# Two-layer hybrid trunk on one core: the weight sums of six P pairs of layer two formed next to their products instead of being read from a copy in DRAM

## The chip, the core and the metric

The kernel runs on one core of one Trainium2 chip. The metric is the device time of one execution in microseconds (us). Five engines work side by side, each through a list of instructions of its own, in order: PE (TensorE, the matrix products), DVE (VectorE), ACT (ScalarE), POOL (GpSimd) and SP (SyncE). SP and POOL do nothing here but start DMA transfers, so a transfer that must wait for its place holds up every transfer that stands behind it on the same engine.

## The reference

Two layers work on x of 2048 tokens by 1024 channels, all in float32. Cut to what matters:

```python
for l in range(DEPTH):                      # DEPTH = 2
    shift, scale, gate = jnp.split(silu(c) @ w_ada[l] + b_ada[l], 3, axis=-1)
    h = rms_norm(x, g_pre[l]) * (1.0 + scale[:, None, :]) + shift[:, None, :]
    proj = h @ w_in[l]                      # 1024 -> 3072: u_a, b_a, c_a, gate_a, u_p, gate_p
    y_a = b_a * causal_depthwise_conv(c_a * u_a, w_conv[l]) * jax.nn.silu(gate_a)
    y_p = causal_multiscale_pool(u_p, w_pool[l], pool_scale[l]) * jax.nn.silu(gate_p)
    y = jnp.concatenate([y_a, y_p], axis=-1) @ w_out[l]
    x = x + gate[:, None, :] * rms_norm(y, g_post[l])
```

## The kernel before

**Blocks.** The tokens are cut into two blocks of 1024, so there are four (layer, block) units: (0,0), (0,1), (1,0), (1,1), counted from zero. Below, "layer two" is layer 1, and "the second block" is (0,1). Each unit is an in phase (h times w_in, then convolution, pooling and gates) and an out phase (y times w_out). Float32 operands are split into a high and a low part, and three matmuls take the place of one: (high, high), (high, low), (low, high).

**Two forms of the in phase.** `in_phase` computes all column groups of w_in with plain products: unit (0,0) entirely and the first half of (0,1). `in_seven` takes two column groups of 128 as a pair and forms them with seven products of half size in place of eight (Winograd's form). The pairs are P (u_p and gate_p), A (u_a and c_a) and B (b_a and gate_a), for four groups each. The list `PAIRS` runs P0, A0, B0, P1, A1, B1 and so on to B3. Each of the seven products is 12 matmuls.

**Weights of a pair.** The seven products need three plain quarters of the weights (A11, A12, A22) and four sums of quarters (S1 to S4). Class `Sevenths` delivers them to slots, in two ways:

- not "made": the four sums come ready, high and low, from a DRAM copy (`sums`), 512 KB each, on POOL's queue (L740); the three quarters come raw, 256 KB each, on SP's queue (L729), then ACT makes the high part (L777) and DVE the low part (L787);
- "made": four raw quarters come on SP's queue (L729), DVE forms the sums (`add`, L758 to L765, four operations), ACT makes seven high parts and DVE seven low parts.

Within a pair's steps, weights are loaded 6 products ahead (`LOAD`), their high parts are made 4 ahead and their low parts 3 ahead (`LOAD, HIGH, SETTLE = 6, 4, 3`). The last six pairs of layer one, computed in (0,1), are made. All twelve pairs of layer two, in (1,0) and (1,1), are not.

**Who makes the DRAM copy.** `sum_task` (L447 to L483) makes half of one pair's sums: four loads of 128 KB into two landing places (L456), four DVE operations (L464 to L467), three ACT copies (L470, L472), three DVE operations (L474, L476), and four stores on POOL's queue (L478, L479, two of L481). The A and B pairs are done in (0,0), the eight tasks of the four P pairs in the `in_phase` of (0,1).

**What else runs in that stage.** `finish_tasks` closes the block before: sixteen tasks, each with two loads into landing places (L1180 from the stored product, L1181 from x), a multiplication and an addition on DVE (L1184, L1186), a square on ACT (L1197), a sum on DVE (L1200) and a store on POOL's queue (L1191). The two landing places come free when DVE has summed and when the store has landed. Ahead of the finish tasks stand 16 fills and 8 mix tasks with a landing place each.

**What sets the order.** Each engine's list is written out as the Python runs (`manual_schedule`). `Paced` strews the background tasks between the product steps ("turns", one per k, six matmuls): at each turn it adds to a credit the tasks' whole DVE time, as estimated in the code, over the number of turns (8 * 12 - 24 = 72), and issues steps while the credit lasts; two tasks are begun at a time and the loads of one more are issued ahead. Its turns begin after turn 13, where the opening ends. At the 72nd of its turns it issues all that is left. `between(many, few)` spreads one list evenly in another. In the plain in phase, the weights of half a column group (`Weights`, L202, L211, L221) are loaded four halves ahead of their use and settled (low part made) two halves ahead, in a half's second turn; a half is four turns, so DVE makes a low part seven turns before PE takes it up.

**Pools.** `working(t, r, l, w, v)` sets how many buffers each pool has; the third is the number of landing places, the second that of the half-size scratch tiles, the fourth that of the raw weights. At the end of a block of layer two `block_end` loads back stored y tiles (L953) through landing places and splits them (L185, L188), three per product step, and loads the first out weights (L202) behind them on SP's queue.

Of the kernel before, what the change touches and what calls it, by code (L numbers as in the profile page):

```python
# [12 lines left out]
P = 128  # L13
# [9 lines left out]
NCG = 4  # L23
# [10 lines left out]
def trunk(ctx: ExitStack, tc: tile.TileContext, xt, c, wada, vec, rcp, win, wupt, wpool, wout, out):  # L34
# [5 lines left out]
    @contextmanager  # L40
    def working(t, r, n, w, v):

        with ExitStack() as st:
            for name, bufs in (("t", t), ("r", r), ("l", n), ("w", w), ("v", v)):
                if bufs:
                    held[name] = st.enter_context(tc.tile_pool(name=name + str(t), bufs=bufs, reuse_waits="tile"))
            yield
# [5 lines left out]
    def tmp(name, dtype=F32):  # L53
        return held["t"].tile([P, HALO + TB], dtype, tag="t", name=name)
# [4 lines left out]
    def landing(name, dtype=F32):  # L59
        return held["l"].tile([P, HS], dtype, tag="l", name=name)  # L60
# [48 lines left out]
    class Work:  # L109
# [5 lines left out]
        def __init__(self):  # L115
            self.q = []
# [314 lines left out]
    PAIRS = [(kind, i) for i in range(NCG) for kind in ("P", "A", "B")]  # L431
# [7 lines left out]
    def sum_task(l, n, u, wide):  # L439

        kind, i = PAIRS[n]
        rs = []
        cols = slice(u * 2 * P, (u + 1) * 2 * P)
        pair = lambda t: t.rearrange("p (a b) -> p a b", b=2 * P)  # L447

        def load():
            if wide:  # L450
                both = tmp("raw01", F32R)
            for h in (0, 1):
                rs.append(pair(both[:, h * HS : (h + 1) * HS] if wide else landing(f"raw{h}", F32R)))
                for row in (1, 0):
                    src = w_src(l, PAIR_OF[kind][row], i)[:, h * KH + 2 * u : h * KH + 2 * u + 2]
                    nc.sync.dma_start(rs[h][:, 1 - row].bitcast(F32).rearrange("p (a b) -> p a b", b=P), src)  # L456

        def steps():
            r0, r1 = [t.bitcast(F32) for t in rs]
            x, xh = pair(half("s13", F32R)), pair(half("s13h", F32R))  # L460
            xf = x.bitcast(F32)
            tt = nc.vector.tensor_tensor
            a21, a11, a22, a12 = r0[:, 0], r0[:, 1], r1[:, 0], r1[:, 1]
            tt(xf[:, 0], a21, a22, op=ALU.add)  # L464
            tt(xf[:, 1], a11, a21, op=ALU.subtract)
            tt(r0[:, 1], xf[:, 0], a11, op=ALU.subtract)
            tt(r1[:, 1], a12, r0[:, 1], op=ALU.subtract)  # L467
            yield 4 * 0.4
            yield None
            nc.scalar.copy(xh, xf)  # L470
            for t in rs:
                nc.scalar.copy(t[:, 0], t.bitcast(F32)[:, 1])  # L472
            yield None
            tt(x, xf, xh.bitcast(F32), op=ALU.subtract)  # L474
            for t in rs:
                tt(t[:, 1], t.bitcast(F32)[:, 1], t.bitcast(F32)[:, 0], op=ALU.subtract)  # L476
            dst = sums[l, n]
            nc.gpsimd.dma_start(dst[:, 0, 0:4:2, cols].bitcast(F32), xh.bitcast(F32))  # L478
            nc.gpsimd.dma_start(dst[:, 1, 0:4:2, cols].bitcast(F32), xf)  # L479
            for m in range(2):  # L480
                nc.gpsimd.dma_start(dst[:, :, 1 + 2 * m, cols].bitcast(F32), rs[m].bitcast(F32))  # L481
            yield E2 + 0.8

        return load, steps, E2 + 2.4
# [225 lines left out]
    SUM = {"S1": 0, "S2": 1, "S3": 2, "S4": 3}  # L710
    LOAD, HIGH, SETTLE = 6, 4, 3

    class Sevenths:


        def __init__(self, l, ring, pairs, made=False):
            self.l, self.ring, self.pairs, self.made = l, ring, pairs, made
            self.ops, self.raws = {}, {}
            self.nm = 7 * len(pairs)
            self.loaded = self.highs = self.settled = 0  # L720
# [11 lines left out]
        def load(self, upto):  # L732
            while self.loaded < min(upto, self.nm):
                m = self.loaded
                n, q = divmod(m, 7)
                a = PRODUCTS[q][0]
                if a in SUM and not self.made:
                    kind, i = self.pairs[n]
                    t = self.place(m)
                    nc.gpsimd.dma_start(t.rearrange("p a b c -> p a (b c)"), sums[self.l, PAIRS.index((kind, i))][:, :, SUM[a]])  # L740
                elif not self.made:
                    self.raws[m] = self.quarter(n, *QUARTER[a])
                elif q == 0:
                    self.raws[m] = self.raws[m + 1] = self.quarter(n, 0, 0)
                    self.raws[m + 2] = self.quarter(n, 1, 0)
                    self.raws[m + 5] = self.quarter(n, 1, 1)
                elif q == 4:
                    self.raws[m] = self.raws[m + 2] = self.quarter(n, 0, 1)
                self.loaded += 1
# [19 lines left out]
        def high(self, upto):  # L769
            self.load(upto)  # L770
            us = 0
            while self.highs < min(upto, self.nm):
                m = self.highs
                if m in self.raws:
                    if self.made:
                        us += self.add(m)
                    nc.scalar.copy(self.place(m)[:, 0], self.raws[m].rearrange("p (a b) -> p a b", b=P))  # L777
                self.highs += 1
            return us
# [676 lines left out]
    mine = lambda kinds: [(n, u) for n, u in units if PAIRS[n][0] in kinds]  # L1456
# [14 lines left out]
    with working(9, 4, 4, 3, 0):  # L1471
        with tc.manual_schedule(engines={E.DVE, E.PE, E.Activation}):
            hrhs, started = start(0)
        with tc.manual_schedule():
# [4 lines left out]
            made = [sum_task(1, n, u, True) for n, u in mine("AB")]  # L1479
# [44 lines left out]

        return ws, closing, done

    with working(5, 6, 5, 6, 2), tc.manual_schedule():
        plain = [(kind, i) for kind, i in IN_ORDER if i < PLAIN]
        pairs = [(kind, i) for kind, i in PAIRS if i >= PLAIN]
        first = in_weights(0, plain, 0, turned(ws.places, 16))  # L1530
        h, fills, opening, hrhs = out_phase(0, 0, y, 0, 1, ws, hplaces, yorder, first, True)
        ring = first.places + hplaces[8 : 8 + KH]
        wts = Sevenths(0, ring, pairs, True)
        later = Later()
        mixes = [mix_task(1, g, n, later) for g in range(NCG) for n in range(2)]
        fins = finish_tasks(0, 0, later)
        sums_ = [sum_task(1, n, u, False) for n, u in mine("P")]
        tasks = between(fills, mixes) + between(fins, sums_)
        in_phase(0, 1, hrhs, tasks, later, None, None, first.places, wts, first, opening, plain)
        hp = {}  # L1540
        for k in range(KH):
            hp["B11", k], hp["B21", k], hp["B22", k] = hplaces[k], hplaces[KH + k], hplaces[12 + k]
        it = iter(yorder)
        for name in ("T2", "T3", "T1", "T4"):
            for k in range(KH):
                hp[name, k] = next(it)
        ws, closing, done = block_end(0, 1, hp, ring, pairs, False, (3, 2, 3, 2, 2, 2))
        kept = in_seven(0, 1, h, [], None, [], later, wts, closing, pairs)
        y, yorder, wplaces, hplaces, _ = done(kept)
    with working(5, 8, 6, 3, 2), tc.manual_schedule():  # L1550
        for n, (l, b) in enumerate(blocks[2:], 2):
            lplaces = yorder[4:]
            ring = wplaces[1:] + yorder[:4] + wplaces[:1]
            wts = Sevenths(l, ring, PAIRS)
            h, fills, opening, _ = out_phase(*blocks[n - 1], y, l, b, ws, hplaces, lplaces, wts)
            hp = {}
            it = iter(hplaces)
            for k in range(KH):
                for name in ("B11", "T1", "T3", "T2"):
                    hp[name, k] = next(it)  # L1560
            it = iter(lplaces)
            for name in LATE:
                for k in range(KH):
                    hp[name, k] = next(it)
            later = Later()
            tasks = finish_tasks(*blocks[n - 1], later)
            if (l, b) == (1, 0):
                tasks = between(tasks, [ada_task(1, 2 * KT + k) for k in range(KT)])
                tasks += [call_task(lambda: ada_fin(1, 2, 0, KT), 0.3)]
            last = n + 1 == len(blocks)  # L1570
            ws, closing, done = block_end(l, b, hp, ring, PAIRS, last, (3, 3, 3, 3, 2, 0))
            kept = in_seven(l, b, h, fills, opening, tasks, later, wts, closing, PAIRS)
            y, yorder, wplaces, hplaces, spare = done(kept)
            if last:
                out_last(l, b, y, ws, spare)
# [41 lines left out]
```

## Time and profile before

| what | value |
|---|---|
| median of 3 runs | 1449.65 us (1447.68 to 1452.13) |
| the profiled execution | 1452.83 us, of which its span is 1451.0 us |
| mean granted TensorE clock of the span | 0.98 |
| PE busy | 1385.0 us, 95% of the span |
| DVE busy | 984.0 us, 68% |
| ACT busy | 523.8 us, 36% |
| POOL busy | 227.9 us, 16% |
| moved by DMA | 306.97 MB, mean 212 GB/s |

A busy share is an average over stages with different limits; it does not say in which stage PE waits. A wait is put down by the profile to what came last. The granted clock is given as a part of the full 2.4 GHz; the chip's other level is 1.2 GHz, so a stretch between 0.5 and 1.0 was spent partly at each.

### The profile page before, as it was taken

Reading aid. Unit: us, or ns where it says so; the run is one execution under the profiler, and the core shown is the slowest. Engines: PE = TensorE matmul, PEld = TensorE weight load, DVE = VectorE, ACT = ScalarE, POOL = GpSimd, SP = SyncE. Lnnn points to the kernel's source line nnn. Section 1 sums busy time; section 2 is a strip of 40 time slices with the busy share of each in tenths; the row PEclk is TensorE's granted clock in tenths of the full one; section 3 lists DMA queues with packets and bytes.
Section 4 is the critical chain, followed back from the end, with each engine's and each line's share of the span. In section 5 each row is a group of like instructions: output and inputs, shape, how many; then the busy total and the mean of one; then the engine's idle time right before and its main releaser. Section 6 shows DMA issues by size and latency. Waiting matters only on the chain.

```text
span 1451.0 us, 18013 instructions
## 1 busy us (share of the span) xinstructions
PE 1385.0 (95%) x6178; PEld 1134.8 (78%) x6178; DVE 984.0 (68%) x1645; ACT 523.8 (36%) x905; POOL 227.9 (16%) x365
## 2 busy tenths in 40 slices
PE   8999999999999676999999999999999999999996
PEld 4778887888887465788788888888888888888796
DVE  7765978876656466687776767677775756657555
ACT  5333442244554222322665422212656311112521
POOL 0001222211102222000022222121022111211000
PEclk9999999999999898999999999999999999999998
DMA  8516988865637676322566988687567787877422
GB/s 310 178 44 205 330 279 270 269 228 202 219 114 252 204 242 217 131 73 102 167 210 217 293 272 252 220 278 247 195 232 252 235 253 211 252 240 230 160 91 88
DMA packets 149598, 306.97 MB, mean 212 GB/s; under 512 B 16641, under 2 KB 33025, under 8 KB 149506
## 3 DMA queue, kind: packets, MB, share of 16 engines
q1 hardware_dynamic: 100658, 179.44, 38.0%
q0 software_dynamic: 48848, 126.38, 26.0%
q8 instruction: 48, 0.79, 0.2%
q14 instruction: 44, 0.36, 0.1%
HBM read 225.54 MB, written 80.22 MB: 211 GB/s over the span
## 4 chain that ended last, share of the span: by engine, by line
PE 74%; DVE 8%; issue 8%; DMA 7%; ACT 2%; POOL 1%; SPq 1%; DVEq 0%; POOLq 0%; ACTq 0%
PE ps_in L868 37%; PE ps_out L395 22%; PE ps_in L395 13%; DMA raw<-win 2%; DMA late<-late 1%; DVE ws L221 1%; DMA fin<-xt 1%; DVE y L188 1%; DMA adaw<-wada 1%; DMA raw<-wout 1%; DMA ws<-sums 1%; PE ps_stat L1321 0%; PE ps_warm L1304 0%; DVE win L497 0%; PE ps_wu L421 0%
## 5 line engine op out<-in xcount | busy, mean ns | idle before, releaser
L868 PE MATMUL ps_in<-h,ws 128*128 128x512 f32 x2520 | 572.8, 389 | 0.6 <-DMA ws<-sums 0.6
L868 PEld LDWEIGHTS ps_in<-h,ws 128*128 128x128 f32 x2520 | 472.9, 188 | 99.3 <-DMA ws<-sums 1.0
L395 PE MATMUL ps_in<-h,ws 128*128 128x512 f32 x1392 | 335.9, 402 | 32.3 <-DVE ws L221 28.0
L395 PE MATMUL ps_out<-y,ws 128*128 128x512 f32 (+1 forms) x1728 | 354.6, 366 | 2.9 <-ACT ws L211 1.2
L395 PEld LDWEIGHTS ps_out<-y,ws 128*128 128x128 f32 x1728 | 298.4, 189 | 58.4 <-DVE ws L221 1.9
L395 PEld LDWEIGHTS ps_in<-h,ws 128*128 128x128 f32 x1392 | 269.3, 195 | 92.5 <-DVE ws L221 30.9
L221 DVE TENSOR_TENSOR ws<-raw,ws 128x512 fp32r<-128x512 f32 x122 | 83.3, 687 | 71.0 <-ACT ws L211 71.0
L211 ACT CAST ws<-raw 128x512 fp32r<-128x512 f32 x122 | 74.3, 619 | 121.9 <-PE ps_in L395 44.5
L777 ACT CAST ws<-raw 128x512 fp32r<-128x512 f32 x108 | 64.7, 618 | 122.2 <-PE ps_in L868 45.8
L740 POOL DMA_DIRECT2D ws<-sums x96 | 67.8, 707 | 207.2 <-PE ps_in L868 185.2
L395 PE MATMUL ps_in<-h,w 128*128 128x512 f32 x336 | 81.8, 402 | 5.3 <-DVE h L387 2.8
L395 PEld LDWEIGHTS ps_in<-h,w 128*128 128x128 f32 x336 | 63.5, 191 | 22.7 <-DVE h L387 3.6
L787 DVE TENSOR_TENSOR ws<-raw,ws 128x512 fp32r<-128x512 f32 x108 | 74.0, 685 | 4.7 <-ACT ws L777 4.7
L1067 POOL DMA_DIRECT2D ysp<-yg x48 | 26.2, 546 | 221.4 <-ACT yg L1066 220.6
L1186 DVE TENSOR_TENSOR fin<-fin 128x512 f32<-128x512 f32 x48 | 32.9, 686 | 31.8 <-DMA fin<-xt 31.7
L891 ACT COPY v<-ps_in 128x512 f32<-128x512 f32 x30 | 17.6, 588 | 101.9 <-PE ps_in L868 101.9
L912 ACT ACTIVATE second<-second 128x1024 f32<-128x1024 f32 x20 | 21.2, 1062 | 87.3 <-DVE second L906 84.0
L1197 ACT ACTIVATE fin<-fin 128x512 f32<-128x512 f32 x28 | 17.7, 631 | 92.8 <-DVE fin L1186 63.9
L267 DVE SCALAR_TENSOR_TENSOR adaw<-adaw,cb 128x512 f32<-128x512 f32 x64 | 42.7, 686 | 12.3 <-DMA adaw<-wada 12.3
L906 DVE TENSOR_TENSOR second<-ps_in,v 128x512 f32<-128x512 f32 x20 | 13.8, 690 | 43.2 <-PE ps_in L868 43.2
L1075 DVE TENSOR_TENSOR acc<-acc,sq 128x512 f32<-128x512 f32 x42 | 28.5, 691 | 19.9 <-ACT sq L1072 19.9
L1066 ACT ACTIVATE yg<-ps_out,gg 128x512 f32<-128x512 f32 x48 | 33.1, 689 | 13.8 <-PE ps_out L395 13.7
(191 smaller groups left out, 1345.8 us busy)
## 6 DMA issues: line engine op xcount, KB each, us to landing
ws<-sums POOLq DMA_DIRECT2D x96, 512.0 KB, 7.4
raw<-win SPq DMA_DIRECT2D x122, 256.0 KB, 5.1
adaw<-wada SPq DMA_DIRECT2D x64, 256.0 KB, 5.1
raw<-wout SPq DMA_DIRECT2D x64, 256.0 KB, 4.8
sums<-raw POOLq DMA_DIRECT2D x48, 256.0 KB, 5.7
ysp<-yg POOLq DMA_DIRECT2D x48, 256.0 KB, 3.6
fin<-ysp SPq DMA_DIRECT2D x48, 256.0 KB, 5.3
yraw<-yin SPq DMA_DIRECT2D x42, 256.0 KB, 4.0
```

What stands on the lines that cost most here:

```text
L211: nc.scalar.copy(self.ws[m][:, 0], self.raws[m].rearrange("p (a b) -> p a b", b=P))
L221: nc.vector.tensor_tensor(t[:, 1], raw, t[:, 0].bitcast(F32), op=ALU.subtract)
L267: nc.vector.scalar_tensor_tensor(w[n], w[n], 1.0, cb[:, n * HS : (n + 1) * HS], op0=ALU.mult, op1=ALU.mult, accum_out=m[:, l, j : j + 1])
L395: nc.tensor.matmul(ps[s], lhsT=ws[k // KH][:, wi, k % KH, :], rhs=rhs(k, ri, s), start=first and (wi, ri) == PASSES[0], stop=last and (wi, ...
L740: nc.gpsimd.dma_start(t.rearrange("p a b c -> p a (b c)"), sums[self.l, PAIRS.index((kind, i))][:, :, SUM[a]])
L777: nc.scalar.copy(self.place(m)[:, 0], self.raws[m].rearrange("p (a b) -> p a b", b=P))
L787: nc.vector.tensor_tensor(t[:, 1], raw, t[:, 0].bitcast(F32), op=ALU.subtract)
L868: nc.tensor.matmul(ps, lhsT=ops[m][:, wi, k, :], rhs=h[hn][k][:, ri, :], start=p < 4 and k == 0 and (wi, ri) == (0, 0), stop=k == KH - 1 a ...
L1066: nc.scalar.activation(t, ps[s], AF.Copy, scale=gg[:, l, j : j + 1])
L1067: nc.gpsimd.dma_start(ysp[l, b][:, j, s * HS : (s + 1) * HS], t)
L1075: tt(accs[s], accs[s], q, op=ALU.add)
L1186: nc.vector.tensor_tensor(e[1], e[1], e[0], op=ALU.add)
```

## The change

The six sum tasks of P1, P2 and P3 leave the second block, and with them their copies in DRAM; P0's two stay. In both blocks of layer two the pairs P1, P2 and P3 are now made: whether a pair is made is asked pair by pair. The pool counts change at two places: in the second block landing places go from 5 to 6 and raw weight buffers from 6 to 5; in layer two's stage the half-size tiles go from 8 to 7, landing places from 6 to 5 and raw weight buffers from 3 to 5.

```diff
+    SPOT = [("P", i) for i in range(1, NCG)]
+
     class Sevenths:
-        def __init__(self, l, ring, pairs, made=False):
-            self.l, self.ring, self.pairs, self.made = l, ring, pairs, made
+        def __init__(self, l, ring, pairs, made):
+            self.l, self.ring, self.pairs, self.made = l, ring, pairs, [p in made for p in pairs]
...
-                if a in SUM and not self.made:
+                if a in SUM and not self.made[n]:
...
-                elif not self.made:
+                elif not self.made[n]:
...
-                    if self.made:
+                    if self.made[m // 7]:
                         us += self.add(m)
...
-    with working(5, 6, 5, 6, 2), tc.manual_schedule():
+    with working(5, 6, 6, 5, 2), tc.manual_schedule():
...
-        wts = Sevenths(0, ring, pairs, True)
+        wts = Sevenths(0, ring, pairs, pairs)
...
-        sums_ = [sum_task(1, n, u, False) for n, u in mine("P")]
+        sums_ = [sum_task(1, n, u, False) for n, u in mine("P") if PAIRS[n] not in SPOT]
         tasks = between(fills, mixes) + between(fins, sums_)
...
-    with working(5, 8, 6, 3, 2), tc.manual_schedule():
+    with working(5, 7, 5, 5, 2), tc.manual_schedule():
...
-            wts = Sevenths(l, ring, PAIRS)
+            wts = Sevenths(l, ring, PAIRS, SPOT)
```

In SP's list, where the finish tasks of the second block begin, before (`fin` are the two loads of a finish task, `raw_...` of 128x256 the four of a sum task, `raw` of 128x512 the plain weights):

```order
L1180 DMA fin<-ysp_0_131 128x512
L1181 DMA fin<-xt 128x512
L456 DMA raw_3906<-win 128x256
L456 DMA raw_3906<-wu_0_92 128x256
L456 DMA raw_3909<-win 128x256
L456 DMA raw_3909<-wu_0_92 128x256
L1180 DMA fin<-ysp_0_131 128x512
L1181 DMA fin<-xt 128x512
L202 DMA raw<-win 128x512
L1180 DMA fin<-ysp_0_131 128x512
L1181 DMA fin<-xt 128x512
```

And the same engine around the first of the two sum tasks that are left (the lines of the file stand two further down):

```order
L1182 DMA fin<-ysp_0_131 128x512
L1183 DMA fin<-xt 128x512
L202 DMA raw<-win 128x512
L1182 DMA fin<-ysp_0_131 128x512
L1183 DMA fin<-xt 128x512
L456 DMA raw_4107<-win 128x256
L456 DMA raw_4107<-wu_0_92 128x256
L456 DMA raw_4110<-win 128x256
L456 DMA raw_4110<-wu_0_92 128x256
L202 DMA raw<-win 128x512
```

Before, a sum task follows every second finish task; now one stands behind the eighth and one behind the sixteenth.

In DVE's list, in pair B0 of unit (1,0), where the weights of P1 are prepared, before (`adaw` belongs to a background task, `ws` are the low parts of weights):

```order
L901 TENSOR_TENSOR second<-ps_in,second 128x512
L1200 TENSOR_TENSOR xacc<-xacc,fin 128x512
L787 TENSOR_TENSOR ws<-raw,ws 128x512
L267 SCALAR_TENSOR_TENSOR adaw,mod<-adaw,cb 128x512
L906 TENSOR_TENSOR second<-ps_in,v 128x512
L916 TENSOR_TENSOR cv<-ps_in,cv 128x512
L926 TENSOR_TENSOR v<-ps_in,v 128x512
```

And the same stretch after the change:

```order
L903 TENSOR_TENSOR second<-ps_in,second 128x512
L1202 TENSOR_TENSOR xacc<-xacc,fin 128x512
L789 TENSOR_TENSOR ws<-raw,ws 128x512
L760 TENSOR_TENSOR s_6733<-raw 128x512
L761 TENSOR_TENSOR raw<-raw 128x512
L762 TENSOR_TENSOR raw<-s_6733,raw 128x512
L267 SCALAR_TENSOR_TENSOR adaw,mod<-adaw,cb 128x512
L789 TENSOR_TENSOR ws<-raw,ws 128x512
L908 TENSOR_TENSOR second<-ps_in,v 128x512
L918 TENSOR_TENSOR cv<-ps_in,cv 128x512
L789 TENSOR_TENSOR ws<-raw,ws 128x512
L928 TENSOR_TENSOR v<-ps_in,v 128x512
```

Three additions and two low parts have come between the same background and product operations; a fourth addition (L767) and two more low parts follow in the next steps.

## Rows read from the trace of the kernel before

**Rows 1.** Busy by stretch: length, PE, PEld, DVE, ACT, POOL, PEclk, DMA, GB/s.
```profile
311.81:398.85 87.04, 87.04 (x385) 72.10 (x385) 55.07 (x77) 48.51 (x79) 11.93 (x22) 1.00 0.61 212
398.85:454.02 55.17, 52.09 (x260) 43.55 (x260) 29.89 (x46) 27.54 (x49) 5.14 (x9) 1.00 0.47 156
454.02:593.14 139.12, 102.98 (x392) 80.84 (x391) 79.64 (x141) 36.19 (x71) 33.71 (x52) 0.87 0.67 228
808.55:926.03 117.48, 117.48 (x520) 97.27 (x519) 82.94 (x139) 29.80 (x49) 25.02 (x39) 1.00 0.84 257
1126.92:1325.56 198.64, 198.64 (x878) 164.50 (x877) 121.32 (x177) 36.66 (x59) 41.32 (x64) 1.00 0.75 229
```

**Rows 2.** PE's largest wait, 454 to 593 us: us in total, times, longest.
```profile
PE ps_in L395 <- DVE ws L221: 28.0, 6, 7.1
```

**Rows 3.** PE's instructions in order of time, with the wait before them in brackets.
```profile
502.92 7.50 PE L395 MATMUL ps_in<-h,ws 128*128 128x512 f32 x24 [7.11 <-DVE ws L221]
...
531.85 15.98 PE L395 MATMUL ps_in<-h,ws 128*128 128x512 f32 x68 [1.80 <-DVE ws L221]
```

**Rows 4.** Busy time of the stretches behind these two waits, columns as in rows 1.
```profile
502.92:510.42 7.50, 7.50 (x24) 5.70 (x24) 2.96 (x5) 0.52 (x2) 3.92 (x6) 0.75 0.61 245
531.85:547.82 15.97, 15.97 (x68) 12.60 (x68) 12.48 (x21) 4.42 (x9) 3.37 (x6) 1.00 0.64 211
```

**Rows 5.** The longest wait of DVE in total, 454 to 593 us.
```profile
DVE fin L1186 <- DMA fin<-xt: 31.7, 10, 7.1
```

**Rows 6.** Waits of SP's DMA queue, 454 to 593 us.
```profile
SPq L1181 <- DMA x<-fin: 26.8, 7, 6.0
SPq L456 <- DMA sums<-raw: 17.3, 5, 5.2
SPq L1181 <- DMA sums<-raw: 16.2, 2, 11.1
```

**Rows 7.** DMA issues, 455 to 600 us: count, size, median us to landing.
```profile
x<-fin POOLq DMA_DIRECT2D x16, 256.0 KB, 3.4
sums<-raw POOLq DMA_DIRECT2D x16, 256.0 KB, 4.7
fin<-ysp SPq DMA_DIRECT2D x14, 256.0 KB, 3.9
```

**Rows 8.** The sum tasks' last stores: min/median/max ns, first and last start.
```profile
L481 POOL DMA_DIRECT2D sums<-raw x16: 706/768/822, 470.4 to 583.9; - x16
```

**Rows 9.** Costliest groups of the page: busy, mean ns of one.
```profile
L787 DVE TENSOR_TENSOR ws<-raw,ws 128x512 fp32r<-128x512 f32 x108 | 74.0, 685 | 4.7 <-ACT ws L777 4.7
...
L777 ACT CAST ws<-raw 128x512 fp32r<-128x512 f32 x108 | 64.7, 618 | 122.2 <-PE ps_in L868 45.8
```

**Rows 10.** Busy time over one pair, B0 of (1,0), columns as in rows 1.
```profile
837.50:856.60 19.10, 19.10 (x86) 15.83 (x85) 13.29 (x21) 4.45 (x7) 3.25 (x5) 1.00 0.81 261
```

**Rows 11.** End of (1,1), in order of time on DVE, SP, ACT and PE.
```profile
1334.68 1.89 DVE L188 TENSOR_TENSOR y<-yraw,y 128x512 fp32r<-128x512 f32 x3
...
1336.97 0.90 SPq L202 DMA_DIRECT2D raw<-wout  x2
...
1341.37 0.62 ACT L211 CAST ws<-raw 128x512 fp32r<-128x512 f32 x1 [2.75 <-DMA raw<-wout]
...
1350.01 3.49 PE L395 MATMUL ps_out<-y,ws 128*128 128x512 f32 x14 [0.45 <-DVE y L188]
...
1354.71 5.58 PE L395 MATMUL ps_out<-y,ws 128*128 128x512 f32 x22 [1.20 <-ACT ws L211]
```

**Rows 12.** End of (1,0), in order of time on DVE, SP and PE.
```profile
1024.42 0.69 DVE L221 TENSOR_TENSOR ws<-raw,ws 128x512 fp32r<-128x512 f32 x1 [2.86 <-ACT ws L211]
...
1019.10 0.90 SPq L202 DMA_DIRECT2D raw<-wout  x2
...
1027.03 8.32 PE L395 MATMUL ps_out<-y,ws 128*128 128x512 f32 x36
```

**Rows 13.** DMA issues of the page that bear on the end of a block.
```profile
yraw<-yin SPq DMA_DIRECT2D x42, 256.0 KB, 4.0
```

## The prediction

> **What bounds the kernel now.** I first read the busy time by stretch. In layer two PE is busy for the whole of the long stretches at a granted clock of 1.00 (117.48 of 117.48 us, 198.64 of 198.64 us), so nothing can be won there; things can only be lost. In the out phase of (0,0) 384 matmuls take 87.04 us, 0.2267 us each: that is the price of a matmul with no wait. The second block's plain in phase is different: from 454.02 to 593.14 us there are 139.12 us, PE is busy for 102.98 of them and the clock is 0.87 [rows 1]. It has 384 matmuls of products there (576 of the stage, less the 192 that stand before 454.02) and 4 of statistics: 388 * 0.2267 = 88.0 us. So 51.1 us are lost, 36.1 idle and 15.0 through matmuls that run longer. From 398.85 to 454.02 PE is idle for 3.1 us.
>
> Next I read who is waited for. PE waits for low weight parts from DVE, 28.0 us in 6 waits [rows 2]. DVE stands in its list before a finish task's addition, whose x tile has not come: 31.7 us in 10 waits [rows 5]. The tile is late because SP could not start the load: its queue waits for a landing place that a store must free, 26.8 us for the finish tasks' store and 17.3 + 16.2 us for the sum tasks' [rows 6]. So the chain runs landing place, SP, DVE, low part, PE, and this stage is bound by the turnover of five landing places.
>
> **The clock.** Behind a wait of 7.11 us [rows 3] 24 matmuls took 7.50 us at a mean clock of 0.75, 0.31 us each; behind one of 1.80 us 68 took 15.97 us at 1.00 [rows 4]. A long wait costs a second time, through a stretch partly at 1.2 GHz. That is where the 15.0 us come from, and they go with the waits.
>
> **The second block, worked out.** A landing place of a finish task is held at least for a load (3.9), two DVE operations (1.4), the issue and landing of a store (0.5 and 3.4) [rows 7]: 9.2 us. A sum task holds its two for a load, some 1.7 us of DVE, 1.4 of ACT, 1.4 of DVE, 2.9 of POOL issues and 4.7 to land [rows 7], about 16 us. Each task takes two places.
>
> - Before: five places are 2.5 tasks in flight. 16 * 9.2 + 8 * 16 = 275 us, over 2.5 is 110 us; the stretch in which all 24 run is about 131 us, from the stage's 454 to the last sum store's issue at 584 and a little more [rows 8], 1.19 times that. The pace asks for less: the background DVE time is 74.4 us by the code's estimates (fills 11.2, mixes 4.8, finish 33.6, sums 24.8), 1.03 us per turn, and the 24 tasks fill about 57 turns of 6 * 0.2267 = 1.36 us, 77 us. Places are short by half, and the stage stretches.
> - After: 16 * 9.2 + 2 * 16 = 179 us over three tasks in flight is 60 us, times 1.19 is 71 us. The background time is 55.8 us, 0.775 us per turn; fills and mixes take 21 turns from turn 14 on, and the 18 tasks the 51 from there to turn 86, 69 us. So places and pace are about even, and DVE may be late by seven turns (9.5 us) before PE notices, the statistics' products by five (6.8 us).
>
> So nearly all of the 51.1 us should go. I leave 4 us, for the waits at the statistics and the second sum task, which is issued last, and expect 1 of the 3.1 us before 454 back: gain 48. The bounds of what stays: 0; and, if each task in flight still takes what it did (131 * 2.5 / 24 = 13.6 us, so 18 * 13.6 / 3 = 82 us against 69), 13 us and some 5 for the clock, 18. Traffic should be no limit: 139.12 us at 228 GB/s are 31.7 MB, six tasks of 1.5 MB go, and 22.3 MB in 92 us are 242 GB/s, below the 257 GB/s that stand beside an undisturbed PE [rows 1].
>
> Five raw buffers in place of six: of the made pairs' four quarters the third then waits about one product (2.7 us) for its buffer. It is needed three products after its turn and the loads are short, so I take 0; uncovered it would delay DVE, not PE, whose weights are settled three products ahead.
>
> **Layer two, six pairs made on the spot.** Each pair adds four additions and four low parts on DVE, 8 * 0.685 = 5.5 us, and four copies on ACT, 2.5 us [rows 9]. It removes four transfers of 512 KB from POOL's queue and adds one of 256 KB to SP's. DVE is busy 13.29 of 19.10 us in the pair in which P1 of (1,0) is prepared, ACT 4.45 [rows 10]; with 5.5 us more DVE has 0.3 us left. Weights are settled about three products (8.2 us) before use, and the background tasks yield, since each step's budget of 2.5 us is first charged with the weights. I take 0. If the cover goes, all 5.5 us of each pair are on the path: 33 us for six. In (1,1) the background is smaller.
>
> **Five landing places at the end of a block.** Here the change makes something later. Three y tiles are loaded per product step while three wait and three are being split. With six places the third load of a step waits for a tile split in that same step; with five it waits for the first tile of the next step, 2.7 us later. Behind it in SP's list stand the first two out weights. In (1,1) they are issued at 1336.97, ACT waits 2.75 us for them, and PE then waits for y and for weights, 0.45 and 1.20 us: the chain is tight, and 2.7 us go straight to PE [rows 11]. In (1,0) they are issued at 1019.10, and the first low part is ready at 1025.1 against a start of the out phase at 1027.03 [rows 12]: 1 to 2 us of the 2.7 are covered. Together about 4. The bounds: 0, if other waits cover both, and 2 * (2.7 + 4.0) = 13, if a whole landing [rows 13] is exposed on top at both ends.
>
> The Trainium skill, page "Perfetto Trace Analysis", section "Optimization Strategy", says that a gap that repeats on the engine that should be saturated can mean too few buffers. The second block's rows agree; by the same rule taking a place away in layer two may bring such gaps back there, which is the upper bound of 13 above. In the long stretch it should not bite: 24 tasks in 188 us leave 19.6 us per turnover at five places.
>
> The smaller scratch pool (seven for eight) I take at 0: two tiles are held through a stage, a product row of the out phase (10.9 us) uses seven, each for 4 to 5 us. If it binds, ACT waits some 2 us for a store once per block, off the path.
>
> **The sum.** 1452.83 - 48 + 4 = 1408.8 for the profiled execution, which stands 3.2 us above the median; from the median 1449.65 - 44 = 1405.7, so 1406.
>
> **The rivals.**
>
> - Finish tasks hold the queue by themselves. Their own store accounts for the 26.8 us of SP's waits; if only the sum tasks' share, six eighths of 33.5, goes, 25 us are won, 4 paid: about 1429. For it: the largest single wait is theirs. Against it: the sixth place, which lets a task load both tiles at once. The Trainium skill, page "TensorE: Matmul & The Clock Gate", section "HAM oscillation", says that stalls repeated between short bursts bring the half clock back each time; the rows agree behind the long wait and not behind the short one [rows 4]. By that rule even halved waits would keep most of the 15 us, a result like this rival's.
> - DVE becomes the bound in layer two's P pairs. The three pairs of (1,0) with little left, or all six: 16 to 33 us given back, 1422 to 1439. For it: 0.3 us of room [rows 10]. Against it: three products of lead, and a budget that holds the background back.
> - Slower: the finish tasks' own loop is the whole limit, and the freed places only let them queue earlier. Then the stage keeps its 139 us and the end of layer two's blocks costs 4 to 13: 1454 to 1463. It decides if the 16 tasks still take 131 us, 8.2 us each; against it stands that their bare turnover is 9.2 us for three tasks at once.
> - The ends of the blocks cost nothing and the stage loses nothing: 1449.65 - 52 = 1398.
>
> **How the numbers follow.** A change below 0.3% (4.3 us) cannot be told from none here. Chances: forecast 0.62 (1399 to 1415), finish loop 0.17, DVE in layer two 0.09, nothing lost at all 0.07, slower 0.03, and 0.02 for mixtures that end within 0.3%. So faster 0.95, same 0.02, slower 0.03. The range takes in the bounds of what stays (0 and 18), the block ends (0 and 13, of which the upper half is unlikely) and part of the finish loop: 1397 to 1424.
>
> **What would show it.** Right: 398.85 to 593.14 falls from 194 us to about 146, the clock is 0.97 or more in it, PE's waits for low parts fall below 8 us, SP's waits for `sums` nearly vanish; in layer two the P pairs stay at 19.0 us each with DVE near 18.8; at both block ends the out weights are issued about 2.7 us later against the y tiles, and PE waits 1 to 3 us. Wrong: long waits of DVE for x tiles remain (finish loop); PE idles inside layer two's pairs (DVE).

## The result and the profile after

The changed kernel takes 1401.72 us (median of 4 runs, 1399.37 to 1401.90), the kernel before 1449.59 us (4 runs): a ratio of 0.9665, 95% interval 0.9647 to 0.9683. That is 47.9 us less; 44 were forecast. The profiled execution took 1401.63 us, its span 1399.9 us.

Where it came from is read from PE's timeline, at the borders of the stages. Of the kernel before (start, length, instruction, tiles, count):

```profile
592.98 114.40 PE L868 MATMUL ps_in<-h,ws 128*128 128x512 f32 x504
707.22 9.91 PE L395 MATMUL ps_out<-y,ws 128*128 128x512 f32 x43
...
796.53 11.08 PE L868 MATMUL ps_in<-h,ws 128*128 128x512 f32 x48
...
1027.03 87.20 PE L395 MATMUL ps_out<-y,ws 128*128 128x512 f32 x384
1114.07 2.88 PE L868 MATMUL ps_in<-h,ws 128*128 128x512 f32 x12
...
1344.40 5.16 PE L395 MATMUL ps_out<-y,ws 128*128 128x512 f32 x22
```

Of the changed kernel, the same view:

```profile
311.47 87.20 PE L395 MATMUL ps_out<-y,ws 128*128 128x512 f32 x384
...
541.08 114.40 PE L870 MATMUL ps_in<-h,ws 128*128 128x512 f32 x504
655.32 17.39 PE L395 MATMUL ps_out<-y,ws 128*128 128x512 f32 x76
...
743.00 8.48 PE L870 MATMUL ps_in<-h,ws 128*128 128x512 f32 x36
751.89 3.03 PE L870 MATMUL ps_in<-h,ws 128*128 128x512 f32 x12 [0.40 <-DMA ws<-sums]
...
974.80 87.20 PE L395 MATMUL ps_out<-y,ws 128*128 128x512 f32 x384
1061.84 2.88 PE L870 MATMUL ps_in<-h,ws 128*128 128x512 f32 x12
...
1292.27 1.38 PE L395 MATMUL ps_out<-y,ws 128*128 128x512 f32 x5
```

The differences of these starts, with the plain in phase of the second block from the busy rows ([rows 1] and below), give the lengths (us):

| stretch | before | after | difference |
|---|---|---|---|
| (0,1) plain in phase | 194.3 | 142.6 | -51.7 |
| (0,1) pairs | 114.24 | 114.24 | 0 |
| out phase of (0,1) | 89.31 | 87.68 | -1.6 |
| (1,0) pairs | 230.50 | 231.80 | +1.3 |
| out phase of (1,0) | 87.04 | 87.04 | 0 |
| (1,1) pairs | 230.33 | 230.43 | +0.1 |
| last out phase, to the end of the span | 106.6 | 107.6 | +1.0 |

Nearly the whole gain lies in the one stage. The changed kernel there (columns as in rows 1):

```profile
454.00:541.08 87.08, 87.08 (x388) 72.10 (x387) 62.52 (x100) 26.98 (x51) 17.10 (x29) 1.00 0.73 244
398.51:541.08 142.57, 140.42 (x650) 116.65 (x648) 91.95 (x145) 56.19 (x101) 21.63 (x37) 1.00 0.66 220
```

From 454 us on PE is busy for 87.08 of 87.08 us at a clock of 1.00. The 139.12 us of rows 1 are 52 us shorter; 1.4 of these are six matmuls that were done before 454 us here. The waits in the stage, by the engine, the line and what it waits for (us in total, times, longest):

```profile
PE ps_wu L421 <- DMA wupt<-wupt: 2.1, 2, 1.2
...
DVE fin L1188 <- DMA fin<-xt: 4.0, 4, 1.5
...
SPq L1183 <- DMA x<-fin: 10.4, 4, 6.0
SPq L1182 <- DMA x<-fin: 9.1, 5, 3.2
...
SPq L1183 <- DMA sums<-raw: 0.9, 1, 0.9
```

PE's wait for low parts [rows 2] is not in the list any more. DVE waits 4.0 us for x tiles where it waited 31.7 [rows 5]. SP still waits for the finish tasks' stores, about 20 us, but its waits for `sums` [rows 6] have shrunk from 33.5 us to 1.4, of which the line shown is the longest. So the queue is still slowed by landing places, but PE no longer waits for anything that comes late through them.

In layer two, two stretches of 19.10 us in which P pairs are prepared (the first is the same stretch as rows 10):

```profile
784.40:803.50 19.10, 19.10 (x86) 15.83 (x85) 16.63 (x27) 6.11 (x11) 1.30 (x3) 1.00 0.55 190
...
841.70:860.80 19.10, 19.10 (x86) 15.83 (x85) 17.11 (x29) 6.42 (x11) 0.59 (x1) 1.00 0.65 207
```

DVE does 16.63 us of work there instead of 13.29, and PE is full. The ends of the blocks, (1,0) first (start, length, engine, instruction):

```profile
968.53 0.90 SPq L202 DMA_DIRECT2D raw<-wout  x2
...
972.97 0.69 DVE L221 TENSOR_TENSOR ws<-raw,ws 128x512 fp32r<-128x512 f32 x1 [3.56 <-ACT ws L211]
...
1286.04 0.90 SPq L202 DMA_DIRECT2D raw<-wout  x2
...
1290.16 0.62 ACT L211 CAST ws<-raw 128x512 fp32r<-128x512 f32 x1 [2.96 <-DMA raw<-wout]
...
1293.97 4.26 PE L395 MATMUL ps_out<-y,ws 128*128 128x512 f32 x17 [0.32 <-DVE ws L221]
1298.80 3.46 PE L395 MATMUL ps_out<-y,ws 128*128 128x512 f32 x14 [0.56 <-DVE y L188]
1303.49 38.81 PE L395 MATMUL ps_out<-y,ws 128*128 128x512 f32 x180 [1.22 <-ACT ws L211]
```

Measured back from the start of the out phase, the first out weights are issued 6.27 us ahead in (1,0), where it was 7.93 [rows 12], and 6.23 us ahead in (1,1), where it was 7.43 [rows 11]: 1.7 and 1.2 us later. The wait of 0.32 us for low parts of the weights, behind the phase's first five matmuls, was not there before.

### The profile page after: what moved, and what is told of

Its sections match the earlier page's. It is cut to its first block, busy times and chain, and to the rows that moved or that the text cites. A ratio compares the mean times of both kernels' runs of the same rounds, so it can differ in the third digit from the quotient of the medians.

```text
span 1399.9 us, 17906 instructions
## 1 busy us (share of the span) xinstructions
PE 1370.2 (98%) x6178; PEld 1126.4 (80%) x6178; DVE 995.9 (71%) x1651; ACT 529.7 (38%) x911; POOL 193.7 (14%) x317
## 4 chain that ended last, share of the span: by engine, by line
PE 83%; DVE 7%; DMA 5%; issue 2%; ACT 2%; SPq 0%; POOL 0%; DVEq 0%; ACTq 0%; POOLq 0%
PE ps_in L870 38%; PE ps_out L395 23%; PE ps_in L395 21%; PE ps_wu L421 1%; DMA raw<-win 1%; DVE y L188 1%; DVE ws L221 1%; DMA adaw<-wada 1%; DMA ws<-sums 1%; DMA ysp<-yg 1%; DMA raw<-wout 1%; PE ps_warm L1306 0%; DMA sums<-s13h 0%; DVE adaw L267 0%; PE ps_stat L1323 0%
## 5 line engine op out<-in xcount | busy, mean ns | idle before, releaser
L870 PE MATMUL ps_in<-h,ws 128*128 128x512 f32 x2520 | 573.2, 389 | 0.8 <-DMA ws<-sums 0.8
L395 PE MATMUL ps_in<-h,ws 128*128 128x512 f32 x1392 | 323.1, 392 | 0.0
L779 ACT CAST ws<-raw 128x512 fp32r<-128x512 f32 x126 | 75.6, 619 | 218.4 <-DMA raw<-win 58.5
L221 DVE TENSOR_TENSOR ws<-raw,ws 128x512 fp32r<-128x512 f32 x122 | 83.2, 687 | 69.8 <-ACT ws L211 68.1
L211 ACT CAST ws<-raw 128x512 fp32r<-128x512 f32 x122 | 74.4, 620 | 148.6 <-PE ps_in L395 70.2
L789 DVE TENSOR_TENSOR ws<-raw,ws 128x512 fp32r<-128x512 f32 x126 | 86.3, 685 | 9.5 <-ACT ws L779 9.1
L742 POOL DMA_DIRECT2D ws<-sums x72 | 51.0, 709 | 169.4 <-PE ps_in L870 110.5
L1186 DVE TENSOR_TENSOR fin<-fin,ry 128x512 f32<-128x512 f32 x48 | 32.8, 684 | 1.9 <-DMA fin<-ysp 1.9
L427 POOL DMA_DIRECT2D wu<-wk x16 | 9.0, 566 | 171.1 <-ACT wk L426 170.9
```

The costliest lines, as they stand in the source:

```text
L211: nc.scalar.copy(self.ws[m][:, 0], self.raws[m].rearrange("p (a b) -> p a b", b=P))
L221: nc.vector.tensor_tensor(t[:, 1], raw, t[:, 0].bitcast(F32), op=ALU.subtract)
L395: nc.tensor.matmul(ps[s], lhsT=ws[k // KH][:, wi, k % KH, :], rhs=rhs(k, ri, s), start=first and (wi, ri) == PASSES[0], stop=last and (wi, ...
L789: nc.vector.tensor_tensor(t[:, 1], raw, t[:, 0].bitcast(F32), op=ALU.subtract)
L870: nc.tensor.matmul(ps, lhsT=ops[m][:, wi, k, :], rhs=h[hn][k][:, ri, :], start=p < 4 and k == 0 and (wi, ri) == (0, 0), stop=k == KH - 1 a ...
L1186: nc.vector.tensor_tensor(e[0], e[0], ry[l, b, s], op=ALU.mult)
```

## The experiments

The theory is the prediction's: the second block's in phase is as long as the turnover of its landing places, and loses nothing once that fits the pace of the matmuls. The rivals are that the sixth place alone is the cure, that the number of sum tasks alone decides, and that layer two pays for it somewhere. There were twelve runs; two of them repeat a kernel.

**place_alone**: the kernel before with six places.

```diff
-    with working(5, 6, 5, 6, 2), tc.manual_schedule():
+    with working(5, 6, 6, 5, 2), tc.manual_schedule():
```

> The kernel before with one edit: six landing places and five raw buffers in the second block; all eight sum tasks stay, layer two is as before. Theory (turnover of landing places): three tasks in flight instead of two and a half, 275 / 3 * 1.19 = 109 us of turnover against 77 us of pace; late by 32, of which 9.5 are hidden; with the slow clock about 26 us stay of the 51. That is 1422 to 1430, with SP still waiting for the stores of the sum tasks. Rival 1 (the sixth place alone is the cure): 1397 to 1403, the stage at about 143 us. Rival 2 (the sum tasks' work is the limit, by their count): no gain, 1446 to 1452.

Measured 1430.77 us, ratio 0.9857 (0.9830 to 0.9884), just above the theory's 1422 to 1430. Its stage:

```profile
392.30:569.08 176.78, 152.30 (x649) 123.19 (x648) 109.06 (x187) 63.72 (x119) 38.66 (x61) 0.92 0.69 231
```

What DVE and PE waited for in it:

```profile
DVE s L464 <- DMA raw<-win: 28.7, 7, 6.9
DVE fin L1186 <- DMA fin<-xt: 5.3, 5, 3.6
...
PE ps_in L395 <- DVE ws L221: 15.8, 5, 6.1
```

The sixth place wins 17.5 us of the stage. With it the finish tasks no longer wait for their x tiles (5.3 us instead of 31.7); DVE now stands before the sum tasks' first addition, 28.7 us where it was 13.9. The wait has moved from one customer of the landing places to the other. Both rivals fall: the place is not the whole cure, and with all sum tasks in place there is a gain.

**tasks_alone**: the changed kernel with five landing places and six raw buffers in the second block.

> The changed kernel with one edit: the second block keeps five landing places and six raw buffers. The six sum tasks are gone and layer two makes its pairs. Theory (turnover): two and a half tasks in flight, 179 / 2.5 * 1.19 = 85 us of turnover against 70 us of pace; late by 15, of which 9.5 are hidden; with the clock about 7 us lost, and the end of the second block waits for y as before, 1.6 us: 1407 to 1413. Rival 1 (the place is the cure): more than 1425. Rival 2 (the count of sum tasks alone): 1400 to 1404.

Measured 1408.97 us, ratio 0.9706 (0.9690 to 0.9723), inside the theory's 1407 to 1413 and outside both rivals'. Its stage, and under it the longest of DVE's waits there:

```profile
397.08:545.92 148.84, 141.87 (x650) 116.31 (x648) 91.95 (x145) 56.09 (x101) 21.37 (x37) 1.00 0.64 209
```
```profile
DVE fin L1188 <- DMA fin<-xt: 16.6, 10, 4.0
```

Taking out the six sum tasks wins 45.5 us of the stage by itself, the place another 6.3 on top. The two gains don't add: 17.5 + 45.5 = 63.0, and both together won 51.7.

**made_p3**, **made_p2_p3**, **made_all_p**: the changed kernel with six, four and no sum tasks left; the list of made pairs starts at 3, 2 and 0.

```diff
-    SPOT = [("P", i) for i in range(1, NCG)]
+    SPOT = [("P", i) for i in range(3, NCG)]
```

> The changed kernel with P3 alone made in layer two: six sum tasks stay in the second block, with its six landing places. Theory (turnover, a threshold): 16 * 9.2 + 6 * 16 = 243 us over three tasks in flight, times 1.19, is 96 us against 75 us of pace; late by 21, 9.5 hidden, with the clock 13 us lost. Since eight sum tasks with six places lost 34 us where the theory said 26, 13 to 18: a plain in phase of the second block of 156 to 161 us. Rival (a fixed price per sum task: 34 us over the six tasks, 5.7 us each): four more tasks than in the changed kernel, 23 us, a stage of 165 us.

> The changed kernel with P2 and P3 made in layer two: four sum tasks stay in the second block, with six landing places. Theory (turnover, a threshold): 211 us over three tasks, times 1.19, is 84 us against 73 us; late by 11, of which 9.5 are hidden: 2 to 6 us lost, a stage of 145 to 149 us. Rival (a fixed price per sum task): two more tasks, 11 us, a stage of 154 us.

> The changed kernel with all four P pairs made in layer two: no sum task is left in the second block. Theory (the turnover was already within the pace): the stage stays at 141 to 143 us, and layer two's first pair, whose quarters now come at the start of the block, costs 0 to 3 us there. Rival (each sum task still has its price): two fewer tasks, 3 to 11 us less, but no less than the 139 us that the matmuls take: a stage of 139 us.

**seven_places**: the kernel before with `working(5, 6, 7, 4, 2)` in the second block.

> The kernel before with seven landing places and four raw buffers in the second block; all eight sum tasks stay. Theory (turnover): 275 us over three and a half tasks in flight, times 1.19, is 94 us against 77 us of pace; late by 17, 9.5 hidden, with the clock 8 us lost, or up to 15 by what six places lost beyond the theory: a stage of 151 to 158 us. Rival 1 (places matter in pairs, since a task takes two: seven do what six do): 177 us. Rival 2 (four raw buffers starve the weights): more than 177 us.

Measured (2 runs each) 1418.50, 1410.59, 1397.11 and 1420.19 us; ratios 0.9769 (0.9734 to 0.9804), 0.9714 (0.9686 to 0.9743), 0.9622 (0.9594 to 0.9650) and 0.9781 (0.9752 to 0.9809). The four stages in this order:

```profile
398.27:555.61 157.34, 146.08 (x650) 119.99 (x648) 103.34 (x173) 61.22 (x113) 32.92 (x53) 0.97 0.71 239
```
```profile
397.67:549.59 151.92, 143.20 (x649) 117.90 (x648) 97.57 (x159) 58.96 (x107) 27.29 (x45) 0.98 0.68 227
```
```profile
397.91:537.86 139.95, 139.95 (x649) 116.79 (x648) 86.78 (x131) 54.09 (x95) 15.64 (x29) 1.00 0.61 201
```
```profile
396.67:557.99 161.32, 148.06 (x649) 120.81 (x648) 108.58 (x187) 63.87 (x119) 38.68 (x61) 0.95 0.74 253
```

With no sum task PE is full for the whole stage: 140.0 us is what the matmuls take. Against it the eight kernels can be laid side by side. "Turnover" is the prediction's bare one, 9.2 us for each of 16 finish tasks and 16 us for each sum task, over half the number of places; "slow clock" is PE's busy time above 139.95 us.

| kernel | places | sum tasks | turnover, us | stage, us | lost, us | of it slow clock |
|---|---|---|---|---|---|---|
| made_all_p | 6 | 0 | 49 | 140.0 | 0 | 0 |
| after | 6 | 2 | 60 | 142.6 | 2.6 | 0.5 |
| made_p2_p3 | 6 | 4 | 70 | 151.9 | 12.0 | 3.3 |
| tasks_alone | 5 | 2 | 72 | 148.8 | 8.9 | 1.9 |
| seven_places | 7 | 8 | 79 | 161.3 | 21.4 | 8.1 |
| made_p3 | 6 | 6 | 81 | 157.3 | 17.4 | 6.1 |
| place_alone | 6 | 8 | 92 | 176.8 | 36.8 | 12.4 |
| before | 5 | 8 | 110 | 194.3 | 54.3 | 15.1 |

Sorted by turnover the loss rises almost in step, though places and tasks differ (the rows of 70 and 72 us, and those of 79 and 81, stand the other way round): from some 58 us on, about one microsecond is lost for each of turnover (within 7 us in every row; this line was drawn after the runs). That is what the theory says, and neither rival can: kernels with the same places lose 0 to 37 us, kernels with the same eight tasks 21 to 54.

As sizes the expectations did worse. tasks_alone and made_p3 came out inside theirs; place_alone, seven_places (161.3 us for 151 to 158) and made_p2_p3 (151.9 for 145 to 149) lost more, and made_all_p (140.0 for 141 to 143) less. The rival of a fixed price per task gave 165, 154 and 139 us for made_p3, made_p2_p3 and made_all_p; they took 157.3, 151.9 and 140.0: the second lies nearer to it than to the theory, the third half-way. It falls by the first, and by the seventh place, which won 15.5 us over six with all eight tasks still there. So places do not count only in pairs either, and four raw buffers did not starve the weights. Of place_alone's 36.8 us the first two tasks taken away give 19.4, the next two 5.4, then 9.4 and 2.6, though each two are the same 10.7 us of turnover: that unevenness is not explained. The last step is the changed kernel's 2.1 us of waits for `wupt` and 0.5 of clock; the waits end at 449.7 and 453.4 us, before the first sum task's loads at 478.2, so they are not its landing places.

No run separates the landing places of a sum task from its own work on DVE. But that work is not what binds: in place_alone's stage DVE is busy for 109.06 of 176.78 us and waits for tiles, and seven_places has the same work in 161.3 us. Nor is it the traffic: seven_places moved the most in a second, 253 GB/s, and lost less than place_alone, which moved 231.

**layer_two_alone** and **pools_alone** price the other half. The first is the changed kernel with the second block as before:

```diff
-    with working(5, 6, 6, 5, 2), tc.manual_schedule():
+    with working(5, 6, 5, 6, 2), tc.manual_schedule():
...
-        sums_ = [sum_task(1, n, u, False) for n, u in mine("P") if PAIRS[n] not in SPOT]
+        sums_ = [sum_task(1, n, u, False) for n, u in mine("P")]
```

> The changed kernel with the second block as it was: all eight sum tasks and five landing places. Six of the eight sets of sums are stored and never read; layer two makes P1, P2 and P3 itself. It prices layer two's half of the change by itself. Theory (the block ends and the additions are hidden but for what the changed kernel's trace shows): +1 to +3 us, 1450 to 1453. Rival 1 (the forecast of 2.7 us later out weights at both ends): +4 or more, 1453.5 to 1458. Rival 2 (the additions of the pairs reach PE, and a gain elsewhere hid it): +16 or more.

The second is the kernel before with `working(5, 7, 5, 5, 2)` in layer two:

> The kernel before with one edit: layer two's stage has seven half-size tiles, five landing places and five raw buffers; nothing is made on the spot there. It prices the smaller pools alone. Theory: +0.5 to +2 us, all of it at the end of (1,1) and the start of (1,0), 1450 to 1452. Rival (the forecast): +4, 1453.5 or more. Second rival: the two more raw buffers help, and the run is even or faster, 1449.

Measured 1453.07 us, ratio 0.9999 (0.9982 to 1.0015), and 1455.20 us, ratio 1.0015 (0.9996 to 1.0033). The second lies in the range of the rival with the forecast's +4, the first between theory and rival. But the runs of each kernel spread over some 12 us, so these times can't tell +1 from +4; the stages of layer two, from one profiled execution each, can. Of layer_two_alone, PE's timeline:

```profile
799.87 11.48 PE L870 MATMUL ps_in<-h,ws 128*128 128x512 f32 x48
...
1031.65 87.24 PE L395 MATMUL ps_out<-y,ws 128*128 128x512 f32 x384
1118.72 11.05 PE L870 MATMUL ps_in<-h,ws 128*128 128x512 f32 x48
...
1348.67 1.31 PE L395 MATMUL ps_out<-y,ws 128*128 128x512 f32 x5
...
1359.70 38.84 PE L395 MATMUL ps_out<-y,ws 128*128 128x512 f32 x180 [1.18 <-ACT ws L211]
```

(1,0)'s pairs take 231.78 us, (1,1)'s 229.95, the last out phase 107.4: +1.3, -0.4 and +0.8 against before. pools_alone, which makes no pair, has +1.0, -0.2 and +1.2. So the six made pairs cost nothing that can be seen, and what layer two pays, about 2 us, is paid for the pools. The forecast's +4 is not borne out.

**after_again**, **made_all_p_again**, **six_in_layer_two**, **all_p_six**, on one chip: the two versions once more, and both with a sixth landing place and four raw buffers in layer two.

```diff
-    with working(5, 7, 5, 5, 2), tc.manual_schedule():
+    with working(5, 7, 6, 4, 2), tc.manual_schedule():
```

> The changed kernel once more, for a comparison on one chip with the version that makes all P pairs: 1399 to 1403, the stage at 141 to 145 us.

> All four P pairs made, once more. If the last two sum tasks cost what the single looks say (2.6 us in the stage and about 1 us at the start of layer two, less 1 at the end), 3 to 5 us under the changed kernel: 1395 to 1399. If that was chance: 1400 to 1402.

> The changed kernel with six landing places and four raw buffers in layer two. Theory (the fifth place taken there costs some 1 us at the start of (1,0) and some 0.8 us at the end of (1,1)): both go back to what they were before, (1,0) 230.5 us and the last out phase 106.6 to 107.0 us; 1398.5 to 1400.5. By the forecast's 4 us at the two block ends: 1397 to 1398. Rival (four raw buffers hold the made pairs up, which have three quarters and an early one of the next pair in them): PE waits inside the P pairs, 1403 or more.

> All four P pairs made and six landing places with four raw buffers in layer two. The last out phase, 109.0 us with all P pairs made and five places, goes to 107 us: 1394 to 1397, the best of all. Rival (the raw buffers): PE waits inside the P pairs, 1400 or more.

Measured (4 runs each):

| kernel | us | lowest to highest | (1,0) pairs | last out phase |
|---|---|---|---|---|
| after_again | 1400.48 | 1399.10 to 1405.76 | 231.04 | 107.6 |
| made_all_p_again | 1397.50 | 1393.39 to 1399.74 | 230.46 | 108.7 |
| six_in_layer_two | 1401.20 | 1398.16 to 1401.41 | 231.38 | 107.3 |
| all_p_six | 1393.19 | 1392.99 to 1398.96 | 230.46 | 106.7 |

The last of them: its plain in phase of the second block, and PE's timeline from its last out phase on:

```profile
395.60:535.64 140.04, 140.04 (x650) 116.72 (x648) 86.85 (x131) 54.21 (x95) 15.70 (x29) 1.00 0.61 201
```
```profile
1284.46 5.26 PE L395 MATMUL ps_out<-y,ws 128*128 128x512 f32 x22
1290.29 3.47 PE L395 MATMUL ps_out<-y,ws 128*128 128x512 f32 x14 [0.57 <-DVE y L188]
1294.97 38.80 PE L395 MATMUL ps_out<-y,ws 128*128 128x512 f32 x180 [1.22 <-ACT ws L211]
```

all_p_six is the best kernel here, a ratio to before of 0.9606 (0.9574 to 0.9638) and 7.3 us under the changed kernel on the same chip, where the two sets of runs nearly touch and don't overlap. The two profiled spans differ by 6.1 us, and 5.9 of them lie in stages that the edits touch: 2.7 in the second block, 0.6 in (1,0), 2.0 in (1,1), of which after_again lost 1.5 in one wait for P0's `sums`, and 0.9 at the end, less 0.3 in the out phase of (0,1). Four raw buffers hold nothing up: in all_p_six PE has no wait in layer two's pairs. The theory on six_in_layer_two did not come true: the last out phase moved by 0.3 us only, the start of (1,0) did not come back, and 1401.20 us is above its 1398.5 to 1400.5.

## Why the prediction was right, point by point

- **What bounds the stage** was right: the turnover of the landing places, through SP and DVE to the low parts, shown by the table of eight kernels and by the waits that went.
- **The second block's gain** was put at 48 us and is 51.7. Of 54.2 us to be had (51.1 and 3.1) the changed kernel leaves 2.1 in PE's waits for `wupt`, just as forecast, and about 0.5 instead of the 4 left "for the waits at the statistics and the second sum task". That term was mis-sized; nothing waits there.
- **The slack** of 9.5 us by which DVE may be late before PE notices made no difference for the changed kernel, which stands at the edge. In the expectations that used it, slack and clock can be told apart: waits alone are the table's loss less its slow clock. In place_alone they cost 24.4 us, where 32 less 9.5 are 22.5, and in made_p3 11.3, where 21 less 9.5 are 11.5. There the slack held, and the slow clock was put too low: 12.4 and 6.1 us, where the expected 26 and 13 in all left some 3.5 and 1.5. In made_p2_p3 and seven_places the waits too were longer than by the slack, 8.7 us for 1.5 and 13.3 for 7.5. So 9.5 us are not a fixed allowance; what decides how much of it holds stays open.
- **The clock** came with the waits, as forecast: 15.1 us before, 0.5 after, PEclk 1.00. The rival that halved waits would keep most of it was right as a mechanism: place_alone cut the time lost in waits from 39.2 to 24.4 us and the slow clock's share only from 15.1 to 12.4. The Trainium skill, page "TensorE: Matmul & The Clock Gate", section "HAM oscillation", says that stalls between short bursts bring the half clock back each time; that run agrees. In the changed kernel it did not come about, since nearly all the waits went.
- **Raw buffers, six to five, at 0**: right; the pairs of (0,1) take 114.24 us in both.
- **Made pairs at 0**: right, but more easily than forecast. DVE has 16.6 to 17.1 us of work in 19.1, not 18.8: the eight extra operations of a pair don't all fall into one pair. Five of them fall into the first stretch, as in the list of DVE shown with the change; a fourth addition and two low parts follow in the next pair.
- **The block ends at +4** is the step that failed. The weights are 1.7 and 1.2 us later, not 2.7. At (1,0) all of it is covered: the out phase starts without a wait. At (1,1) PE's longest wait for weights is 1.22 us where it was 1.20; with six places it is 1.22 too (all_p_six), so that one does not hang on the place. A smaller one does: the 0.32 us at 1293.97. Eight of the nine profiled runs with five places have such a wait, 0.20 to 0.33 us, and none of the five with six; the 14 matmuls behind start 6.53 us into the phase where it was 5.61. So the path that the forecast named is there, at a third of the 2.7 us. What is left is about +1: five places gave 107.2 to 109.0 us for the last out phase in nine profiled runs, six gave 106.6 to 107.3 in five, before and seven_places among them. The place is worth most where P0 is made too: 109.0 and 108.7 us with five, 106.7 with six.
- **Two terms were missing**, of opposite sign; that they nearly cancel is luck. The sixth place of the second block serves the end of (0,1) too: 89.0 to 89.7 us for its out phase with five places (four profiled runs), 87.35 to 87.99 with six (nine), 87.04 with seven (one); the raw buffers changed along with the places. And the first pair of (1,0) lost 1.3 us: 0.8 before its statistics, where PE waits 0.40 us for `sums`, and 0.5 at them. It is not the landing place (six_in_layer_two has 231.38 us). It is gone where P0's sums are not loaded at all (230.46 us in three profiled runs). The part at the statistics goes back to the half-size tiles, where the change took one of eight. Their operand `al` lies in such a tile, and DVE waits with it until the store of a `yg` tile, of the same pool, has landed; before and after:

```profile
805.22 1.29 DVE L188 TENSOR_TENSOR al<-acc,ah 128x512 fp32r<-128x512 f32 x2
```
```profile
755.10 0.69 DVE L188 TENSOR_TENSOR al<-acc,ah 128x512 fp32r<-128x512 f32 x1 [1.47 <-DMA ysp<-yg]
```

Seven of the eight profiled runs that have seven such tiles and load P0's sums show this wait, 0.46 to 1.80 us; the eighth shows none. From the first statistics matmul to the next product all eight take 0.1 to 0.9 us longer than the 0.93 of before; the three with eight tiles and the three that do not load the sums do not, though with eight tiles these stores took 10 us and more to land. No run changed the tiles alone. The wait for `sums` stays open: seven_places, with eight tiles, waits 2.0 us there.

The sum, then: -51.7 - 1.6 + 1.3 + 0.1 + 1.0 and 0.2 less in the first block are -51.1 us between the profiled spans, of which the forecast had -44. The median moved by 47.9, since the profiled run of before stood above its median.

## What to carry to other kernels

Where several background tasks share one pool of landing places, add up how long each holds its places, divide by how many fit at once, and compare with the time that the main work gives them: here the excess came back on the path about one to one, the slow clock's share included, and within 7 us. Taking work out of the pool and adding a place act on the same quotient, so their gains don't add. When a pool's size is changed for one stage, look at everything else that uses it in that stage: here the end of the block, which the forecast did not have in view, and a statistics operand that shares its pool with a store.

## What the runs showed that was not expected

A single wait costs about 1.6 times its length, in a stage that no edit touches. The in phase of the first block took 284.7 us in place_alone and 292.0 in layer_two_alone, with the same instructions. In the one run PE passes the first statistics without a wait worth showing, in the other it waits 4.01 us, and the 12 matmuls behind it take 5.29 us, 0.44 each instead of 0.23, some 2.5 us more:

```profile
228.47 0.50 PE L313 MATMUL ps_stat<-al,ones 128*128 128x512 f32 x1
228.81 11.54 PE L395 MATMUL ps_in<-h,ws 128*128 128x512 f32 x50
```
```profile
234.65 0.79 PE L313 MATMUL ps_stat<-al,ones 128*128 128x512 f32 x1 [4.01 <-DVE al L370]
235.24 5.29 PE L395 MATMUL ps_in<-h,ws 128*128 128x512 f32 x12
```

The profiled runs of the other kernels lie between: 285.4 us in pools_alone, which has no such wait either, 288.0 in all_p_six with one of 1.2 us and another, for weights, of 1.85, 290.8 in the changed kernel with one of 3.2. So a run can be some 7 us longer through a stage that all these kernels share, and edits worth 1 to 4 us were read from the stages that they touch, not from the medians.
